# Where the state-space coefficients are computed: tables and coefficients pause in some slots of a two-layer decoder kernel, and coefficients begin 15 slots ahead instead of 9

## The chip, the core and the metric

The kernel runs on one core of a Trainium2 chip. The core has five engines that run side by side and meet through semaphores: TensorE (PE in the profile, with its weight loads as PEld), VectorE (DVE), ScalarE (ACT), GpSimd (POOL) and SyncE (SP), which here only starts weight loads. The metric is the time of one execution in microseconds (us) on the device. Lower is better.

## What is computed

Two identical layers work on 512 tokens of 1024 channels in float32. Each layer normalises its input, multiplies it with one wide matrix, feeds parts of the product to three mixers, and adds the gated sum back:

```python
def hybrid_layer(x, ...):
    h = rmsnorm(x, norm_g)
    proj = h @ w_in            # 8704 columns, split into the 13 parts below
    (rq, rk, rv, rz, sq, sk, sv, sz, cu, cz, ga, gb, gc) = split(proj)
    y_a = retention(rq, rk, rv, ...) * silu(rz)
    y_b = stick_breaking(sq, sk, sv, ...) * silu(sz)
    y_c = s5_ssm(cu, ssm_a_re, ssm_a_im, ...) * silu(cz)
    merged = sigmoid(ga) * (y_a @ proj_a) + sigmoid(gb) * (y_b @ proj_b) + sigmoid(gc) * (y_c @ proj_c)
    return x + merged @ w_out

def stick_breaking(q, k, v, ...):        # 8 heads of 64, strictly causal
    z = q @ k.T * scale
    log_keep = where(causal, log_sigmoid(-z), 0)
    after = cumsum(log_keep, reverse=True) - log_keep
    return where(causal, exp(log_sigmoid(z) + after), 0) @ v

def s5_ssm(u, a_re, a_im, log_dt, b_re, b_im, c_re, c_im, ...):   # 32 groups, 64 complex states
    dt = exp(log_dt)
    ab = exp(dt * a_re) * (cos(dt * a_im), sin(dt * a_im))        # one complex step per state
    bb = (ab - 1) / a * b                                         # input matrices
    h[t] = ab * h[t-1] + bb @ u[t]
    y = Re(c @ h) + d_skip * u ; return gelu(y) * sigmoid(gelu(y) @ w_glu + b_glu)
```

What matters below is that the state-space mixer needs quantities that depend on parameters alone (powers of `ab`, and matrices built from them with `b` and `c`), so they can be computed at any time before they are used.

## The kernel before

**Matrix products.** All large products are made in float32 as three products of split operands (helper `three`): a high part `wh` of the weights, a low part `wl`, and `hh`, `hl` of the activations. A weight unit of 128x1024 is loaded as `raw` by SP, then ACT makes `wh` (line 318) and DVE makes `wl` (recorded by the helper of line 197, as are all counted instructions). Up to four units are made ahead (`W.fill`).

**Slots.** `layer` cuts the products into pieces, of 24 matmuls of 512 columns as a rule, and issues them in a fixed order, `ORDER`. One pass of the loop over `mains` is a slot. Each layer has 108; in each the slots are counted here from 0. Slots 0 to 11 are the columns `sk`, `sq`, `sv`; 12 to 23 are `sz` and `gb`; 24 to 27 are `cu`; then `cz`, `pb`, `gc` and the rest. Everything else is a generator that is put on a calendar (`spawn`) for a slot and is advanced there: in a slot come first the generators due, with their matmuls, then the slot's own piece, then the parts that follow it (`late`), then `W.fill`, and last the background work. Each engine executes its instructions in the order in which they were issued, so an instruction issued late in a slot also stands behind all that came before it on its engine.

**Attention.** `sb_pair` handles two heads at a time; the four pairs begin in slots 11, 15, 19 and 23. For each pair the first slot makes split operands (`qd`, `ks` on ACT, `ql`, `ks` on DVE, and on POOL a memset of `ql` and a copy in `qd`). Then come, slot by slot: scores of the last block of head 0 (tile `z3`); scores of the other blocks of head 0 (`z02`, `z1`); `z3` of head 1 together with the turning of head 0's weights (transposes into `wt`); `z02`, `z1` of head 1; the turning of head 1; the product with `sv` (`sbo`). For each score tile ACT makes two sigmoids, DVE scans one of them (`kp`, line 1051) and multiplies (`w`); the transposes of a turn need all of a head's `w`. So pair 0's first scores are in slot 12, its turns in slots 14 and 16, pair 1's in 18 and 20, pair 2's in 22 and 24, pair 3's in 26 and 28. In slots 15, 19 and 23 the first slot of one pair meets the `z02` and `z1` of the pair before it. Score, turn and transpose results share five PSUM tiles (`ps_sm`).

**Tables and coefficients.** `tables` (layer 0 only) makes the powers of `ab` for both layers with small DVE instructions, into `y`, `fr`/`fi` and `cr`/`ci`; its last two steps, six instructions each, fill `cr` and `ci`. A `Coef` object per layer then makes that layer's matrices: first four loads on ACT's queue (line 672) and eight POOL instructions of 128x512 or 64x512 (`bbr`, `bbi`, `ccr`, `cci`), then four quarters. A quarter is six POOL products and sums (`ab`, `ct`), six DVE instructions (`Tr`, `Ti` from `cr`, `ci`, `fr`, `fi`), six more on POOL (`ca`), and copies. It also puts two generators on the calendar: `transpose_in` (eight transposes on PE and two ACT copies into `win`) and `within` (`pk` on PE, `kk` on DVE, 16 copies into `mt` on POOL and ACT). Quarter q begins no earlier than slot `start + 3 q` and, from quarter 2 on, not before an earlier quarter was used; `start` lies `K["lead"]` slots ahead of the first use of the matrices, which is in slot 33:

```python
starts = [at["cu"] + 3 + K["ssm0"]]      # slot 33
coef.start = starts[0] - K["lead"]       # slot 24
```

Both are the background. After each slot the loop adds background steps while the slot's own estimated load is light, `load["G"] < G_SHARE * load["T"] and load["V"] < V_SHARE * load["T"]` (G is POOL, V is DVE, T is PE). The change is in this condition and in `lead`.

Of the kernel before, what the change touches and what calls it, by code (L numbers as in the profile page):

```python
# [35 lines left out]
K = dict(  # L36

    nw=12, w=4, raw=4, b=48,

    sb0=0, sb_gap=4, ssm0=6, ssm_gap=3, ret0=9, ret_gap=3, x0=-3, x1=2, ret_pre=4, lead=9,  # L40

    g=0.9, v=0.7,

    n1=1, n2=1, q1=1, q2=1, k1=1, k2=2, s1=1, s2=1, s3=1, s4=2, s5=1, s6=1, s7=2, b1=1, b2=1, b3=1,
# [3 lines left out]
G_SHARE, V_SHARE = K["g"], K["v"]  # L48
# [138 lines left out]
def trunk(ctx: ExitStack, tc, x_in, w_in, par_in, bc_in, ng_in, cst_in, rope_in, out):  # L187
    nc = tc.nc
    load = {"V": 0.0, "G": 0.0, "T": 0.0}
# [49 lines left out]
    x1 = dp.tile([S, D], F32, name="x1")  # L239
# [24 lines left out]
    def advance(gen, late):  # L264
        d = next(gen, None)
        if d == 0:
            late.append(gen)
        elif d:
            spawn(gen, now[0] + d)
# [83 lines left out]
    def token_major(lhs, evac):  # L353

        units = []

        def piece(t):
            if not units:
                units.extend(W.take() for _ in range(4))
            ps = pmm()  # L360
            for k in range(8):
                if k == 4 and between:
                    between.pop()()
                w = units[k // 2]
                sl = slice(512 * (k % 2), 512 * (k % 2) + 512)
                three(ps, lhs(k, t), (w[0][:, sl], w[1][:, sl]), k == 0, k == 7)
            if t == NT - 1:
                W.free += 4
            then(evac(t, ps))

        return [lambda t=t: piece(t) for t in range(NT)]
# [109 lines left out]
    G = SSM_GROUPS  # L481
# [328 lines left out]
    def layer(l, last, base):  # L810
# [6 lines left out]
        sq, sk, sv = [], [], [None] * NT  # L817
# [464 lines left out]
        def mk_rhs(k, t):  # L1282
# [7 lines left out]
            sv=token_major(hblock, sv_evac),  # L1290
# [18 lines left out]
        mains, at = [], {}  # L1309
# [7 lines left out]
        def quarters():  # L1317

            q = len(starts) - 1
            if q < 4 and coef.ready >= q and now[0] >= starts[-1]:  # L1320
                spawn(ssm(q), now[0])
                starts.append(now[0] + K["ssm_gap"])
# [10 lines left out]
        def chain(*gens):  # L1333
            for x in gens:
                yield from x

        background = chain(tables(), coef.gen) if l == 0 else coef.gen
        for name, m in mains:
            i = now[0]
            quarters()  # L1340
            late = []
            for gen in due.pop(i, []):
                advance(gen, late)
            m()
            while late:
                advance(late.pop(0), late)
            W.fill()
            while load["G"] < G_SHARE * load["T"] and load["V"] < V_SHARE * load["T"]:
                if next(background, "end") == "end":
                    break  # L1350
                load["G"] += 0.05
            for e in load:
                load[e] = 0.0
            W.free += sum(freed)
            freed.clear()
            now[0] += 1
# [3 lines left out]
    for l in range(L):  # L1360
        base = layer(l, l == L - 1, base)
    while due:
        i = min(due)
# [28 lines left out]
```

## Time and profile before

| | us |
|---|---|
| median of 3 runs | 1310.49 |
| lowest, highest | 1309.92, 1311.50 |
| profiled execution, its own time | 1311.17 |
| its span | 1309.5 |
| PE busy in the span | 1271.7 |
| DVE, ACT, POOL busy | 855.6, 537.6, 382.5 |
| mean granted PE clock | 0.992 |

The page of the profile gives busy time and share by engine; a timeline lists instructions with their start, their length and, in brackets, how long the engine had stood idle before them and what ended that; a view of waits adds these idle times up; a view of windows gives each engine's busy time, with the number of instructions, and the granted TensorE clock, in stretches that one chooses (instructions that reach over an edge count). In the trace a slot can be seen by the matmuls at its start: `z` for scores, `wt` for a turn, `mm` for the slot's own piece. The trace names the scans TENSOR_TENSOR_SCAN; the listing of instructions in the next section names them SCALAR_TENSOR_TENSOR.

### The profile page before, as it was taken

The page shows a single profiled execution, that of the slowest core. Times are in us where ns is not written, and L with a number is a line of the kernel's source. Part 1 is how long each engine was busy: PE and PEld are TensorE (multiplying, and loading weights), DVE is VectorE, ACT ScalarE, POOL GpSimd, SP SyncE. Part 2 cuts the span into 40 slices and gives each one's busy share as a digit, 9 for nine tenths or more (in the row PEclk, how much of TensorE's full clock was granted, in tenths as well). Part 3 has the DMA queues.
Part 4 walks back from the last instruction along what each step waited for, and adds up shares of the span by engine and source line. Part 5 has one row for each costly group of instructions (what it writes and reads, how often), then busy time and mean ns, then how long its engine had stood idle before and what let it go on. Part 6 is the DMA issues. An engine that isn't in the chain of part 4 may idle for free. (4 is left out here: it accounts for less than half of the span.)

```text
span 1309.5 us, 16640 instructions
## 1 busy us (share of the span) xinstructions
PE 1271.7 (97%) x6360; PEld 1048.5 (80%) x6360; DVE 855.6 (65%) x1189; ACT 537.6 (41%) x919; POOL 382.5 (29%) x452
## 2 busy tenths in 40 slices
PE   6989989999999999999999999899999999999998
PEld 5867768788887888888888877788888878888887
DVE  5997678776785438556365576789657844575542
ACT  5445534445343534332244445344534534423311
POOL 3340036638442012000042000584555311210000
PEclk9989989999999999999999999899999999999999
DMA  6232221222322322234433222122241232222342
GB/s 223 90 124 77 65 65 49 81 81 89 119 68 65 104 77 77 81 97 141 161 118 127 81 65 71 43 81 65 84 127 65 65 120 90 65 74 88 97 135 75
DMA packets 37375, 120.05 MB, mean 92 GB/s; under 512 B 4144, under 2 KB 4528, under 8 KB 37296
## 3 DMA queue, kind: packets, MB, share of 16 engines
q1 hardware_dynamic: 29664, 105.40, 25.2%
q10 hardware_dynamic: 7632, 13.59, 3.1%
q8 instruction: 50, 0.82, 0.3%
q14 instruction: 29, 0.24, 0.1%
HBM read 114.78 MB, written 4.19 MB: 91 GB/s over the span
## 5 line engine op out<-in xcount | busy, mean ns | idle before, releaser
L197 DVE TENSOR_TENSOR wl<-raw,wh 128x1024 fp32r<-128x1024 f32 x196 | 251.6, 1294 | 114.6 <-ACT wh L318 111.8
L197 PE MATMUL mm<-hh,wh 128*128 128x512 f32 x640 | 256.0, 400 | 0.0
L197 PE MATMUL mm<-hh,wl 128*128 128x512 f32 x640 | 251.2, 393 | 4.9 <-DVE wl L197 4.9
L197 PE MATMUL mm<-hl,wh 128*128 128x512 f32 x640 | 250.7, 392 | 0.0
L318 ACT ACTIVATE wh<-raw 128x1024 fp32r<-128x1024 f32 x196 | 205.8, 1057 | 86.7 <-PE mm L197 38.9
L197 PE MATMUL mm<-wh,hh 128*128 128x512 f32 x512 | 207.5, 405 | 0.9 <-ACT hh L421 0.9
L197 PE MATMUL mm<-wl,hh 128*128 128x512 f32 x512 | 202.6, 396 | 4.3 <-DVE wl L197 4.3
L197 PE MATMUL mm<-wh,hl 128*128 128x512 f32 x512 | 202.0, 395 | 0.0
L197 PEld LDWEIGHTS mm<-hh,wl 128*128 128x128 f32 x640 | 120.8, 189 | 32.2 <-DVE wl L197 6.3
L197 PEld LDWEIGHTS mm<-hh,wh 128*128 128x128 f32 x640 | 121.0, 189 | 25.1 <-issue 1.6
L197 PEld LDWEIGHTS mm<-hl,wh 128*128 128x128 f32 x640 | 121.0, 189 | 23.5
L197 PEld LDWEIGHTS mm<-wl,hh 128*128 128x128 f32 x512 | 104.5, 204 | 24.5 <-DVE wl L197 7.8
L197 PEld LDWEIGHTS mm<-wh,hh 128*128 128x128 f32 x512 | 104.5, 204 | 19.0 <-ACT hh L421 1.3
L197 PEld LDWEIGHTS mm<-wh,hl 128*128 128x128 f32 x512 | 104.2, 204 | 18.4 <-DVE hl L197 0.3
L1051 DVE TENSOR_TENSOR_SCAN kp<-kp,zero 128x511 f32<-128x511 f32 (+1 forms) x64 | 67.6, 1076 | 26.2 <-ACT kp L1047 26.1
L994 ACT ACTIVATE gate<-mm 128x512 f32<-128x512 f32 x48 | 28.6, 596 | 114.2 <-PE mm L197 114.2
L197 POOL TENSOR_SCALAR ms<-ss 128x8 f32<-128x8 f32 (+3 forms) x56 | 19.1, 341 | 181.5 <-DVE ss L824 100.6
L197 POOL TENSOR_TENSOR rs<-ms,mhalf 128x8 f32<-128x8 f32 (+3 forms) x56 | 64.6, 1154 | 4.7
L1033 POOL CAST qd<-qd 64x512 fp32r<-64x512 f32 x16 | 16.3, 1016 | 134.1 <-ACT qd L1028 133.7
L822 ACT ACTIVATE sq<-mm 128x512 f32<-128x512 f32 x32 | 19.0, 593 | 84.6 <-PE mm L197 84.5
L197 PE MATMUL mm<-wl,mgh 128*128 128x512 f32 x128 | 50.1, 391 | 0.2
L197 PE MATMUL mm<-wh,mgh 128*128 128x512 f32 x128 | 49.9, 390 | 0.0
(253 smaller groups left out, 2263.2 us busy)
## 6 DMA issues: line engine op xcount, KB each, us to landing
raw<-in_w SPq DMA_DIRECT2D x196, 512.0 KB, 3.5
x<-in_x SPq DMA_DIRECT2D x8, 256.0 KB, 7.3
rope<-in_rope ACTq DMA_DIRECT2D x8, 256.0 KB, 3.7
xh<-in_x ACTq DMA_DIRECT2D x8, 256.0 KB, 4.4
x<-xh ACTq DMA_DIRECT2D x8, 256.0 KB, 2.0
xh<-x ACTq DMA_DIRECT2D x8, 256.0 KB, 4.6
out<-xh ACTq DMA_DIRECT2D x8, 256.0 KB, 2.1
gB<-in_ng SPq DMA_DIRECT2D x2, 256.0 KB, 5.8
```

Of the source, the lines that this page charges most:

```text
L197: return f(*a, **k)
L318: ACT(wh, raw, AF.Copy)
L822: ACT(s2, ps, AF.Square)
L994: ACT(sg, ps, AF.Sigmoid)
L1033: nc.gpsimd.tensor_copy(out=qd[h][o, :], in_=qd[h][r, :])
L1051: nc.vector.tensor_tensor_scan(v, v, zero1.to_broadcast([P, n - 1]), 1.0, ALU.mult, ALU.add)
```

## The change

`lead` goes from 9 to 15, so that `start` moves from slot 24 to slot 18 in both layers. And no background step is issued in a set of slots: the slot before pair 0's first and that slot itself (10 and 11), and the six slots from pair 3's first (23 to 28).

```diff
-    sb0=0, sb_gap=4, ssm0=6, ssm_gap=3, ret0=9, ret_gap=3, x0=-3, x1=2, ret_pre=4, lead=9,
+    sb0=0, sb_gap=4, ssm0=6, ssm_gap=3, ret0=9, ret_gap=3, x0=-3, x1=2, ret_pre=4, lead=15,
...
         background = chain(tables(), coef.gen) if l == 0 else coef.gen
+
+        first = at["sv"] + 3 + K["sb0"]
+        turn = first + 3 * K["sb_gap"]
+        quiet = {*range(first - 1, first + 1), *range(turn, turn + 6)}
         for name, m in mains:
...
-            while load["G"] < G_SHARE * load["T"] and load["V"] < V_SHARE * load["T"]:
+            while i not in quiet and load["G"] < G_SHARE * load["T"] and load["V"] < V_SHARE * load["T"]:
                 if next(background, "end") == "end":
                     break
```

No instruction is added or taken away. These are the places where instructions move.

DVE in layer 0, slots 10 to 12, as the difference: `sqk` ends slot 10, `ql` and `ks` are pair 0's operands of slot 11, the four `wl` the weights of slots 12 to 15, `kp` and `w` pair 0's first scan and product of slot 12, and `dbl`<-`cr` the start of the last two steps of the tables.

```order
 L197 TENSOR_SCALAR sqk<-T_882,par_193 128x128 x2
+L197 TENSOR_TENSOR ql_922<-sqk,qd_918 64x512
+L197 TENSOR_TENSOR ks_920<-sqk,ks_920 64x512
+L197 TENSOR_TENSOR ql_923<-sqk,qd_919 64x512
+L197 TENSOR_TENSOR ks_921<-sqk,ks_921 64x512
+L197 TENSOR_TENSOR wl<-raw,wh 128x1024 x4
+L1051 SCALAR_TENSOR_TENSOR kp<-kp,zero_85 128x511
+L197 TENSOR_TENSOR w_1018<-w_1018,kp 128x511
 L197 TENSOR_TENSOR dbl_605<-cr 128x128
 L197 TENSOR_TENSOR dbl_606<-ci 128x128
```

The last 12 table instructions moved from ahead of pair 0's operands to behind its first scan and product, in slot 12; on ACT and POOL the four loads and the eight `bbr`/`bbi`/`ccr`/`cci` instructions moved behind the same point, into slots 12 and 13.

POOL in layer 0, before: from pair 2's operands (slot 19) over pair 3's (slot 23) to the first products of quarter 0 (slot 24).

```order
L1030 MEMSET ql_1454 64x512
L1033 COPY qd_1450<-qd_1450 64x512
L1030 MEMSET ql_1455 64x512
L1033 COPY qd_1451<-qd_1451 64x512
L1030 MEMSET ql_1724 64x512
L1033 COPY qd_1720<-qd_1720 64x512
L1030 MEMSET ql_1725 64x512
L1033 COPY qd_1721<-qd_1721 64x512
L197 TENSOR_TENSOR ab_1855<-bbr,y_re 128x512
L197 TENSOR_TENSOR ct<-bbi,y_im 128x512
L197 TENSOR_TENSOR ab_1855<-ab_1855,ct 128x512
```

The same engine now, from pair 1's last operand (slot 15) to the first products for `ca` (slot 21).

```order
L1033 COPY qd_1179<-qd_1179 64x512
L197 TENSOR_TENSOR ab_1448<-bbr,y_re 128x512
L197 TENSOR_TENSOR ct<-bbi,y_im 128x512
L197 TENSOR_TENSOR ab_1448<-ab_1448,ct 128x512
L197 TENSOR_TENSOR ab_1449<-bbr,y_re 128x512
L197 TENSOR_TENSOR ct<-bbi,y_im 128x512
L1030 MEMSET ql_1463 64x512
L1033 COPY qd_1459<-qd_1459 64x512
L1030 MEMSET ql_1464 64x512
L1033 COPY qd_1460<-qd_1460 64x512
L197 TENSOR_TENSOR ab_1449<-ab_1449,ct 128x512
L751 COPY ca<-ccr 64x8x16
```

Five of quarter 0's products moved from behind pair 3's operands to between pair 1's and pair 2's; the sixth, with the `ca` copies, stands behind pair 2's, and the six products for `ca` and four of quarter 1 follow, all ahead of pair 3's operands. Layer 1 has the same move.

ACT in layer 0 now, slots 21 and 22: `ybh` is the split of pair 1's result, `win` the two copies behind the eight transposes of quarter 0, `wt` the copies of pair 2's first turn.

```order
L1048 ACTIVATE w_1533<-z_1607 128x256
L318 ACTIVATE wh<-raw 128x1024
L994 ACTIVATE gate<-mm 128x512
L284 ACTIVATE ybh<-sbo 128x512
L729 ACTIVATE win_1745<-T_1688 128x512
L729 ACTIVATE win_1747<-T_1693 128x512
L1047 ACTIVATE kp<-z_1698 128x512
L1048 ACTIVATE w_1749<-z_1698 128x512
L1074 ACTIVATE wt_1755<-wt 128x512
L1076 ACTIVATE wt_1534<-wt 128x256
```

The two `win` copies, with their transposes on PE, moved from slot 27 to slot 22, behind a `ybh` that waits for DVE; on DVE, `Tr` and `Ti` (six instructions) moved from slots 25 and 26 to the ends of slots 20 and 21, ahead of that `sbo`.

## Rows read from the trace of the kernel before

**Rows 1.** The page, part 1: busy us, share of the span, instructions.

```profile
PE 1271.7 (97%) x6360; PEld 1048.5 (80%) x6360; DVE 855.6 (65%) x1189; ACT 537.6 (41%) x919; POOL 382.5 (29%) x452
```

**Rows 2.** The waits of PE: engine, line, waited for: us in total, times, longest.

```profile
PE wt L1068 <- DVE w L197: 13.5, 8, 3.1
PE mm L197 <- DVE wl L197: 9.2, 7, 3.3
```

**Rows 3.** Windows: start:end, length, busy (count) of PE, PEld, DVE, ACT, POOL; clock, DMA.

```profile
90.82:97.65 6.83, 5.19 (x12) 4.12 (x13) 5.64 (x6) 4.69 (x6) 2.53 (x3) 0.50 0.06 8
...
186.39:193.22 6.83, 4.82 (x16) 4.27 (x17) 6.53 (x7) 0.98 (x2) 3.19 (x4) 0.50 0.17 49
```

**Rows 4.** Windows as before, one slot each, from its first matmul to the next slot's.

```profile
86.91:99.98 13.07, 8.98 (x29) 6.62 (x29) 11.23 (x9) 4.97 (x6) 6.20 (x6) 0.74 0.38 124
736.18:742.24 6.06, 6.06 (x29) 4.82 (x28) 5.87 (x6) 3.59 (x5) 0.00 (x0) 1.00 0.62 197
137.37:144.47 7.10, 7.10 (x39) 5.87 (x37) 4.85 (x6) 3.80 (x7) 0.00 (x0) 1.00 0.04 14
181.93:197.30 15.37, 9.89 (x39) 8.69 (x37) 11.08 (x10) 3.50 (x6) 7.58 (x7) 0.78 0.22 68
206.65:214.05 7.40, 7.40 (x39) 7.05 (x37) 6.57 (x8) 3.15 (x9) 4.14 (x3) 1.00 0.00 0
222.55:230.63 8.08, 7.14 (x35) 5.29 (x33) 7.25 (x10) 3.55 (x8) 6.04 (x8) 1.00 0.43 135
824.18:839.30 15.12, 9.64 (x38) 8.59 (x37) 11.08 (x10) 3.50 (x6) 7.58 (x7) 0.77 0.22 70
```

**Rows 5.** Timeline of PE: start, length, instruction [idle before <- what ended it].

```profile
152.58 1.20 PE L1068 MATMUL wt<-ident,w 128*128 128x128 f32 x9 [0.68 <-DVE w L197]
185.68 0.30 PE L1068 MATMUL wt<-ident,w 128*128 128x128 f32 x1 [3.07 <-DVE w L197]
188.40 2.18 PE L1068 MATMUL wt<-ident,w 128*128 128x128 f32 x9 [2.41 <-DVE w L197]
207.19 1.26 PE L1068 MATMUL wt<-ident,w 128*128 128x128 f32 x10
225.42 0.50 PE L197 MATMUL mm<-hh,wl 128*128 128x512 f32 x1 [0.79 <-DVE wl L197]
```

**Rows 6.** Windows of DVE alone: length, busy (count, those at the edges too), clock, DMA.

```profile
71.92:73.41 1.49, 1.42 (x7) 1.00 0.00 0
74.53:76.78 2.25, 2.18 (x8) 1.00 0.02 4
78.95:86.02 7.07, 6.90 (x13) 1.00 0.31 107
...
145.87:152.52 6.65, 6.35 (x10) 1.00 0.20 54
176.72:188.34 11.62, 11.29 (x10) 0.92 0.17 52
743.13:746.98 3.85, 3.64 (x7) 1.00 0.05 20
205.81:209.67 3.86, 3.79 (x8) 1.00 0.00 0
```

**Rows 7.** Timeline of POOL: the first and the last of quarter 0's six products; the first `ct` for `bbr`.

```profile
79.16 1.61 POOL L197 TENSOR_TENSOR ct<-br,co_re 128x512 f32<-128x512 f32 x1 [8.62 <-DMA br<-in_bc]
...
179.10 1.40 POOL L197 TENSOR_TENSOR ab<-bbr,y_re 128x512 f32<-128x512 f32 x1
...
186.53 1.52 POOL L197 TENSOR_TENSOR ab<-ab,ct 128x512 f32<-128x512 f32 x1
```

**Rows 8.** Timeline: ACT's table load and `win` copies; PE's slot-14 turn in layer 1.

```profile
95.55 1.28 ACT L1047 ACT_TABLE_LOAD   x1
...
214.89 1.12 ACT L729 ACTIVATE win<-T 128x512 f32<-128x512 f32 x2
...
749.38 1.26 PE L1068 MATMUL wt<-ident,w 128*128 128x128 f32 x10
```

## The prediction

> **What bounds the kernel now.** I began with the page's busy shares. PE is busy for 1271.7 us of a 1309.5 us span [rows 1], so the end is set by PE: the change can win only time in which PE stands idle or runs at half clock. The view of PE's waits tells why it stands idle: turns (`wt`) that wait for the attention's last product `w`, 13.5 us in 8 waits with 3.1 the longest, and pieces that wait for a weight's low part `wl`, 9.2 us in 7 [rows 2]. Both are made by DVE. I then looked for stretches in which the granted clock is down, and found it at 0.50 (the lower level, 1.2 GHz) from 90.82 to 97.65 and from 186.39 to 193.22 [rows 3], each time after such waits; the second has a counterpart in layer 1. PE's work in such a stretch, 5.19 and 4.82 us, would need half the time at the upper level, so each costs 2.6 or 2.4 us on top of the wait.
>
> Slot by slot, against a like slot that is undisturbed [rows 4]: slot 12 of layer 0 takes 13.07 us where layer 1's takes 6.06, so 7.0 are lost. Slot 24 takes 15.37 and 15.12 where slot 26, with the same matmuls, takes 7.40: 8.0 and 7.7 are lost. Slot 28 takes 8.08; a slot with a turn and one piece is slot 18's 7.10 less its `z3`, which is the 0.54 from 206.65 to 207.19 [rows 4, 5], so 6.56, and 1.5 are lost in each layer. These are some 26 us in all, and all of it lies in the region of the change.
>
> The causes are two. In slot 12 the last 12 table instructions stand ahead of pair 0's operands on DVE and run beside POOL's products of layer 0's matrices: from 78.95 to 86.02 they fill 6.90 of 7.07 us [rows 6, 7], where like steps alone take 1.49 (six 128x128) and 2.25 (six 128x256) [rows 6]. In slot 24 the turn waits 3.07 and 2.41 for `w` [rows 5]: the chain from `ql` to the last `w` takes 11.62 us in slot 23 and 6.65 in slot 19 [rows 6]. Slot 23's is the one with six POOL products of 128x512 beside it, from 179.10 to 186.53 plus 1.52 [rows 7]. So a product costs DVE (11.62 - 6.65) / 6 = **0.83 us**, if DVE then reads two operands from on-chip memory. This is the price on which most of the sum rests.
>
> **The change part by part.** No instruction is added, so PE's own work stays, and only waits and clock move.
>
> *Slot 24, both layers.* No POOL product is issued in slots 23 to 28, and those issued before are early enough to be done. The chain should fall from 11.62 to 6.65, and the turn's waits of 3.07 and 2.41 with the half-clock stretch behind them should go. What is late next is a `w` by some 0.2, as in the turn with 0.68 [rows 5], of which slot 23's `pk` covers a part. Gain 7.8 in layer 0, 7.5 in layer 1. A bound from below is the two waits alone with the clock left as it is, about 5.5.
>
> *Slot 28.* The 0.79 for `wl` and the stretched second turn [rows 5] come from the same products and from `Tr`/`Ti` on DVE. With both gone 1.5 is won in each layer; the bounds are 0.8 (only the wait) and 1.5.
>
> *Slots 12 to 14, layer 0.* Slot 12's 7.0 go, since the tables no longer stand ahead of pair 0's operands. But the 12 instructions, at least 1.49 + 2.25 = 3.7 us, now stand behind pair 0's first `w`, ahead of the rest of head 0, and slot 14's turn waits for that. In layer 1, where nothing stands there, its last `w` ends at 746.98 [rows 6] and its turn begins at 749.38 [rows 8]: 2.4 of room. So 3.7 - 2.4 = 1.3 are late if DVE runs free. It won't: the `bbr`/`bbi`/`ccr`/`cci` products, which stood beside the tables before, now stand behind the same point. With five of them beside two-operand work the turn comes 1.3 + 5 x 0.83 = 5.5 late, and after a wait like that the clock drops as in the two stretches above [rows 3], 2.6 more: 8.1 in place of 7.0, a **loss of 1.1**. Bounds: 1.3 alone without a drop of the clock, a gain of 5.7; or six products, ACT's 1.28 table load [rows 8] in the chain and a whole stretch of 6.83 at half clock (3.4), together 11, a loss of 4. I take the upper part since the products are queued just there.
>
> *Slots 16 and 20, both layers.* The turn of slot 20 already comes 0.68 late [rows 5], so each product beside it counts in full. Quarter 0's first product is released in slot 15 and meets the last scans of pair 0, and its sixth stands behind pair 2's operands in slot 19. One product each, 0.8 per slot, so 1.6 lost per layer (bounds 0 and 1.49, the length of a product, from (186.53 + 1.52 - 179.10) / 6 [rows 7]).
>
> *Slot 22, both layers.* This is a new meeting. The `ca` products (six) run beside slots 20 and 21 on DVE, 6 x 0.83 = 5.0, and `Tr`/`Ti` come at the ends of these slots, 3.86 where they run free [rows 6]. DVE has 7.10 - 4.85 = 2.25 of room in a slot like 18 [rows 4], so 6.75 in three. So pair 1's `sbo` is 8.9 - 6.75 = 2.1 late, `ybh` waits for it on ACT, and the two `win` copies (1.12 together [rows 8]) stand behind `ybh`. The third `wt` of pair 2's first turn needs a PSUM tile of `ps_sm` which the first of these copies sets free. PE waits 2.1 + 0.6, and I take **2.5 per layer** (bounds 1 and 3.5, since ACT may have the rest of its slot to catch up, or may have its own copies of `wt` late as well).
>
> *What moves at no price.* The eight `T` transposes and the 16 `pk` go from slot 27 to slots 22 and 23 with the same PE time. The `mt` copies and the later quarters come earlier and hide behind PE as before, since from slot 29 on the order is that of before. Pair 3's POOL operands in slot 23 no longer have products behind them; ahead of them stand quarter 1's, which are due a slot before.
>
> Sum: layer 0 is -1.1 - 1.6 - 2.5 + 7.8 + 1.5 = +4.1, layer 1 is -1.6 - 2.5 + 7.5 + 1.5 = +4.9, so 9.0 us are won. The profiled execution took 1311.17, 1.67 of it outside its span, and would take 1302.2. It lies 0.68 above the median, so on the scale of the runs I forecast 1310.49 - 9.0 = **1301.5**.
>
> **The rivals.**
>
> *The products hardly reach PE.* Slot 14 costs 1.0 and slot 22 costs 0.5, both without a change of clock, and the gain grows by 7.1 + 2 x 2.0 to 20: 1290.4. For it speaks that DVE has 2.25 of room in an average slot, against it that the turn at 152.58 waits without any product beside it [rows 5]. Chance 0.13.
>
> *Slot 22's wait halves the clock as well.* At 186.39 a wait of 3.07 with one of 2.41 went with a drop [rows 3, 5], and 2.5 is near that. A whole stretch costs 6.83 / 2 = 3.4 in each layer, which leaves 9.0 - 6.8 = 2.2: 1308.3, or 1304.9 if it happens in one layer. Chance 0.18.
>
> *Slower: a product holds DVE for its whole length.* The price would be 1.49 in place of 0.83, which is 0.66 more for each: 3.3 in slot 14, 0.7 in each of the four waits of slots 16 and 20, 4.0 in slot 22 of each layer and then also its half clock, 3.4. That is 3.3 + 2.8 + 8.0 + 6.8 = 20.9 against the 9.0: 11.9 slower, 1322.4. It decides once a product costs the chain more than about 1.2. Slot 23's six products added 4.97 to the chain and not 8.9 [rows 6, 7], which speaks against it; but there the chain also has parts that read PSUM, which need not pay, and a denser stretch of two-operand work would pay more. Chance 0.09.
>
> The Trainium skill, page "SBUF — State Buffer", section "Summary: rules for kernel authors", has this rival as a rule: if a DVE instruction has two SBUF inputs while a GpSimd instruction reads SBUF, the one that is issued second fully blocks until the first finishes. By that rule the sum would be the 1322.4 above, and moving products from behind pair 3 to between the other pairs would be a bad exchange. The trace agrees that the two hinder each other, but has 0.83 for a product of 1.49.
>
> That the change doesn't do what it says is excluded by the order of instructions: the products, the tables and the operands do change places in both layers.
>
> **How the numbers follow.** Forecast 0.60, with its own range of 1297 to 1306 from the bounds of slots 14 and 22; the rivals 0.13, 0.18 and 0.09. About 0.2%, 2.6 us, is what a measurement of this kernel can tell from no change, so "the same" is 1307.9 to 1313.1. Faster: nearly all of the forecast (0.58), the first rival, and the one-layer half of the second (0.05), 0.76. The same: the second rival with both layers (0.11) and the rest of the forecast, 0.13. Slower: the third, and 0.02 for a second rival with further waits, 0.11. The range reaches from the first rival's time to a little above the second's, 1290 to 1310; it leaves out the third and about half of the first.
>
> **What the next profile would show.** Right: in both layers slot 24 near 7.4 with no wait of 2 us or more and the clock whole, slot 28 near 6.6, a `wt` wait for `w` of some 5 us in slot 14 of layer 0 with a half-clock stretch behind it, waits of about 1.5 at slots 16 and 20, and in slot 22 a `wt` that waits about 2.5 for ACT's `win`. Wrong: if slots 12 to 14 of layer 0 are clean (the products reach nothing there), if slot 22 has a half-clock stretch, if slot 24 still waits though no product stands beside slot 23, or if anything from slot 29 on has become longer, since nothing of that is in my sum.

## The result, and the profile after

The changed kernel takes 1303.55 us (median of 6 runs), the kernel before 1310.37 beside it: a ratio of 0.9944, 95% interval 0.9933 to 0.9955, so 6 to 9 us faster. One of the six executions took 2571.09 us, for a reason that no run shows; the ratio leaves it out, and the median without it is 1303.42. The profiled execution took 1303.42 in place of 1311.17, its span is 1301.7 in place of 1309.5.

First the page, part 1 (busy us, share, instructions), which answers to [rows 1]:

```profile
PE 1267.4 (97%) x6360; PEld 1048.0 (81%) x6360; DVE 853.3 (66%) x1189; ACT 537.5 (41%) x919; POOL 391.3 (30%) x452
```

Then PE's waits (us in total, times, longest), which answer to [rows 2]:

```profile
PE wt L1068 <- DVE w L197: 12.3, 8, 6.0
...
PE mm L197 <- DVE wl L197: 4.3, 4, 1.6
PE wt L1068 <- ACT win L729: 4.1, 2, 2.1
```

The instruction counts are those of before. The wait for `w` has hardly shrunk in total, but it has moved: its longest is 6.0 where it was 3.1, the one for `wl` has halved, and a new one is there, for ACT's `win`.

Now slot by slot, windows of the changed kernel as in [rows 4] (start:end, length, busy of PE, PEld, DVE, ACT, POOL, clock): slots 12 to 14 of layer 0, then its slots 16, 20, 22, 24 and 28, then slots 16, 20, 22 and 24 of layer 1, and last the two stretches in which the clock is down.

```profile
86.32:115.27 28.95, 22.30 (x98) 17.94 (x97) 24.16 (x30) 11.69 (x18) 9.89 (x9) 0.88 0.37 128
121.90:130.44 8.54, 7.32 (x39) 5.90 (x37) 8.33 (x9) 3.54 (x6) 7.72 (x5) 1.00 0.19 61
153.26:162.45 9.19, 7.51 (x38) 5.97 (x37) 8.88 (x9) 3.60 (x6) 5.65 (x4) 1.00 0.18 57
171.55:181.86 10.31, 8.22 (x47) 6.73 (x45) 9.48 (x10) 4.88 (x9) 7.59 (x8) 1.00 0.16 52
189.18:196.78 7.60, 7.60 (x38) 7.11 (x37) 6.91 (x11) 3.28 (x6) 5.21 (x7) 1.00 0.45 140
220.47:227.14 6.67, 6.67 (x36) 5.42 (x34) 5.14 (x5) 2.50 (x7) 0.00 (x0) 1.00 0.61 182
...
758.74:767.28 8.54, 7.32 (x38) 5.91 (x37) 8.33 (x9) 3.54 (x6) 7.72 (x5) 1.00 0.21 61
790.10:799.10 9.00, 7.51 (x38) 5.97 (x37) 8.69 (x9) 3.60 (x6) 6.24 (x5) 1.00 0.18 58
808.20:820.07 11.87, 9.83 (x46) 7.87 (x45) 10.29 (x10) 4.88 (x9) 9.03 (x8) 0.86 0.15 44
827.39:834.99 7.60, 7.60 (x38) 7.11 (x37) 6.91 (x11) 3.28 (x6) 5.21 (x7) 1.00 0.49 140
...
104.10:110.93 6.83, 4.59 (x16) 3.82 (x17) 6.52 (x9) 1.93 (x3) 0.00 (x0) 0.50 0.00 0
814.07:817.49 3.42, 3.42 (x10) 2.65 (x9) 3.31 (x3) 1.75 (x4) 3.34 (x3) 0.50 0.00 0
```

For comparison, windows of the kernel before that were not shown: its slots 12 to 14, 16 and 20 of layer 0. The first of them begins with a wait of 0.79 for `ks`, so that this wait is counted in it.

```profile
86.91:113.70 26.79, 22.70 (x98) 17.93 (x98) 20.29 (x21) 11.47 (x18) 6.20 (x6) 0.87 0.27 88
120.33:128.28 7.95, 7.34 (x39) 5.90 (x38) 6.55 (x9) 3.59 (x6) 0.52 (x1) 1.00 0.25 69
151.10:159.11 8.01, 7.33 (x39) 5.90 (x37) 6.01 (x8) 3.54 (x6) 0.00 (x0) 1.00 0.31 82
```

Slot 24 has become 7.60 in both layers, with PE busy all of it; slot 28 is 6.67. Against that stand slots 12 to 14 (28.95 against 26.79, where layer 1 takes 19.78), slot 16 (+0.6), slot 20 (+1.2, +1.0) and slot 22, which without its transposes (0.79) is 2.4 longer than the 7.10 of an undisturbed slot in layer 0 and 4.0 in layer 1. The difference between the layers is the second half-clock stretch.

Where the time of slots 14 and 22 goes is seen in the timelines of the changed kernel (start, length, instruction, [idle <- what ended it]): the turn of slot 14, where the wait for `w` now stands, then DVE, ACT and PE of slot 22.

```profile
105.69 0.48 PE L1068 MATMUL wt<-ident,w 128*128 128x128 f32 x1 [6.00 <-DVE w L197]
...
173.60 0.69 DVE L197 TENSOR_TENSOR Ti<-ct,ct 128x512 f32<-128x512 f32 x1
174.21 0.68 DVE L197 TENSOR_TENSOR sbo<-sbo,silu 128x512 f32<-128x512 f32 x1
...
174.93 0.63 ACT L284 ACTIVATE ybh<-sbo 128x512 fp32r<-128x512 f32 x1 [2.59 <-DVE sbo L197]
175.47 1.07 ACT L729 ACTIVATE win<-T 128x512 f32<-128x512 f32 x2
...
176.10 0.33 PE L1068 MATMUL wt<-ident,w 128*128 128x128 f32 x1 [2.09 <-ACT win L729]
```

In slot 22 `Ti` stands ahead of the product into `sbo`; `ybh` waits for that, the `win` copies wait behind `ybh`, and PE's third `wt` waits for the tile that the first copy frees.

### The profile page after: what moved, and what is told of

It reads as the page before. It is cut to its first block, busy times and chain, and to the rows that moved or that the text cites. A ratio compares the mean times of both kernels' runs of the same rounds, so it can differ in the third digit from the quotient of the medians.

```text
span 1301.7 us, 16635 instructions
## 1 busy us (share of the span) xinstructions
PE 1267.4 (97%) x6360; PEld 1048.0 (81%) x6360; DVE 853.3 (66%) x1189; ACT 537.5 (41%) x919; POOL 391.3 (30%) x452
## 5 line engine op out<-in xcount | busy, mean ns | idle before, releaser
L1051 DVE TENSOR_TENSOR_SCAN kp<-kp,zero 128x511 f32<-128x511 f32 (+1 forms) x64 | 59.8, 955 | 21.3 <-ACT kp L1047 21.2
L197 PE MATMUL mm<-wh,mgl 128*128 128x512 f32 x128 | 49.9, 390 | 0.0
```

What stands on the lines that cost most here:

```text
L197: return f(*a, **k)
L1051: nc.vector.tensor_tensor_scan(v, v, zero1.to_broadcast([P, n - 1]), 1.0, ALU.mult, ALU.add)
```

## Undoing one part: the early start alone, the pause without slots 10 and 11

```diff
-        quiet = {*range(first - 1, first + 1), *range(turn, turn + 6)}
+        quiet = set()
```

> Only lead goes from 9 to 15; the pauses are left out. My theory: the earlier start brings the costs in slots 16, 20 and 22 that the changed kernel has (together 4.2 us in layer 0 and 5.5 in layer 1 in its trace), and without the pause the rest of quarter 1 comes in slots 24 to 26 and keeps a part of the loss of slots 24, 26 and 28. Slot 12 of layer 0 loses its 7.0 as in the kernel before. Together about as long as the kernel before or longer, 1308 to 1316 us. Rival, that the early start alone brings the gain (the pauses being needless): 1301 to 1305, with slot 24 near 7.6.

It took 1312.57 us, 1.0014 (1.0004 to 1.0023) of the kernel before: slightly slower, as the theory had it. But one step of that theory fell. Of this run, windows of slots 24 and 26 of layer 0, and then PE's timeline in slot 26:

```profile
186.96:194.84 7.88, 7.61 (x39) 7.11 (x37) 7.51 (x10) 3.28 (x6) 6.51 (x6) 1.00 0.32 85
204.20:219.03 14.83, 10.77 (x47) 8.94 (x46) 9.21 (x11) 4.23 (x11) 10.34 (x9) 0.77 0.00 0
```

```profile
211.16 0.48 PE L1068 MATMUL wt<-ident,w 128*128 128x128 f32 x1 [3.64 <-ACT win L729]
```

Slot 24 is 7.88: it is the earlier start that empties slot 23, not the pause. What the pause does is to keep quarter 1's transposes and `win` copies out of slot 26, where they make the same wait as in slot 22, 3.64 us in each layer, with a half-clock stretch. So the early start pays only together with the pause in slots 23 to 28. The pause without the early start was not run.

```diff
-        quiet = {*range(first - 1, first + 1), *range(turn, turn + 6)}
+        quiet = {*range(turn, turn + 6)}
```

> The changed kernel with background work let into slots 10 and 11 again; slots 23 to 28 stay quiet and lead stays 15. My theory: slots 12 to 14 of layer 0 go back to the kernel before, where slot 12 loses 7.0 and slot 14 nothing, in place of the 9.2 that the changed kernel's trace shows; all else as in the changed kernel. 2.2 us faster than it: about 1301.3. Rival, that the first pause is a gain (it would be if the loss at slot 12 were larger than the one at slot 14): 1305 or more.

1301.11 us, 0.9923 (0.9906 to 0.9940): 2.4 below the changed kernel's median and near the 2.2 expected, but only in part for the reason that I gave. In this run's view of waits PE waits for `ks` in slot 12, where the changed kernel waits 6.00 and 0.65 in slot 14; the half-clock stretch comes with either. Behind that row stand windows of this run: slots 12 to 14 of layer 0 with that wait, slot 20 of layer 0, and slot 22 of layer 1.

```profile
PE z L197 <- DVE ks L197: 4.1, 1, 4.1
...
86.19:113.94 27.75, 23.17 (x99) 17.92 (x98) 21.15 (x25) 11.48 (x18) 3.13 (x5) 0.88 0.26 84
151.94:162.75 10.81, 9.13 (x39) 7.18 (x38) 10.50 (x11) 3.59 (x6) 7.27 (x5) 0.84 0.17 57
807.40:817.66 10.26, 8.22 (x47) 6.73 (x45) 9.43 (x10) 4.88 (x9) 8.67 (x8) 1.00 0.17 51
```

Slots 12 to 14 win 1.2 (27.75 in place of 28.95), not 2.2. The rest comes from slots that I expected to stay as they were: slot 20 of layer 0 loses 1.6, with a new half-clock stretch, and slot 22 wins 1.3 in layer 0 (9.00) and 1.6 in layer 1, where the same wait of 2.04 comes without a half-clock stretch. So the pause in slots 10 and 11 is a loss of about 1.2 by these two traces; that the total came out as forecast is luck. The interval also overlaps that of the changed kernel (0.9933 to 0.9955), as do those of coef_wait and gate_only below: gaps of about 2 us to it are not settled by the times alone.

## What makes slot 14 late: the tables or the products beside them

Layer 0's loads and its six products were held until the end of slot 14, so that the 12 table instructions alone stand behind pair 0's first product.

```diff
+            while l == 0 and now[0] < 14:
+                yield
             raw = [bt(n) for n in ("br", "bi", "ccr", "cci")]
```

> The changed kernel, but layer 0's four loads and six bbr/bbi products wait until the end of slot 14, so that only the 12 table instructions stand behind pair 0's first product. My theory (the POOL products beside it, not the 12 instructions, make slot 14's turn late): the 12 take some 3.5 us in place of 8.85, the turn waits 1.3 in place of 6.0 + 0.65 and no half-clock stretch follows, 7.9 us won there; the products meet slot 15's scans instead and cost up to 2.5 at slot 16's turn. Net gain 4 to 8 over the changed kernel, 1295.5 to 1299.5. Rival, that the 12 instructions themselves are the delay: the wait stays above 4 and the time within 2 us of the changed kernel.

1301.72 us, 0.9926 (0.9911 to 0.9941): 1.8 won, not 4 to 8. Slot 14's half of the theory held: it is 8.59 long, with waits of 0.25 and 0.80. The products' half was too small: slot 16 now takes 14.24, and has taken over the waits (2.71 and 1.31) and the stretch at half clock. Windows of this run's slots 14 and 16, and its timeline of PE in slot 16:

```profile
99.14:107.73 8.59, 7.54 (x38) 5.97 (x37) 7.09 (x10) 3.54 (x6) 2.42 (x2) 1.00 0.67 189
114.36:128.60 14.24, 10.22 (x39) 8.20 (x37) 11.71 (x11) 3.54 (x6) 12.09 (x10) 0.76 0.20 54
```

```profile
117.75 0.30 PE L1070 MATMUL wt<-ident,w 128*128 128x128 f32 x1 [2.71 <-DVE w L197]
```

So the products are what costs, wherever they meet a chain that a turn waits for; the tables alone cost about 1.

## Slot 22: the wait goes, and comes back in slot 24

```diff
-            spawn(transpose_in(), now[0] + K["w1"])
+            spawn(transpose_in(), now[0] + (5 if q == 0 else K["w1"]))
```

> The changed kernel, but quarter 0's eight transposes and two win copies come in slot 25 and not in slot 22, in both layers. My theory (slot 22's turn waits for a PSUM tile that the first win copy frees, and that copy stands behind ybh): the waits of 2.09 and 2.04 go, with the half-clock stretch of layer 1, worth 1.6; slot 22 comes near 7.1 in both layers, about 5.8 us won, 1297.7. Rival, that slot 22's turn would be late anyway for w, since DVE is behind by the same products: waits of 1 us or more for w in slot 22, and a gain under 2 us.

1303.70 us, 0.9943 (0.9928 to 0.9958): no gain. My theory was right for slot 22 and wrong for the time. Windows of slots 22 and 24 of layer 0, and of slot 24 of layer 1:

```profile
171.56:178.66 7.10, 7.10 (x39) 5.87 (x37) 6.30 (x7) 3.92 (x7) 4.42 (x4) 1.00 0.21 75
185.98:197.26 11.28, 9.29 (x39) 8.21 (x37) 9.01 (x14) 3.50 (x6) 5.66 (x8) 0.85 0.31 94
...
823.92:835.10 11.18, 9.24 (x38) 7.98 (x37) 8.94 (x14) 3.50 (x6) 5.66 (x8) 0.85 0.30 95
```

Slot 22 is down to 7.10, and slot 24 up from 7.60 to 11.28 and 11.18. DVE was behind; in the changed kernel PE waits in slot 22, and that wait gives DVE the time to catch up before slot 24. To see what DVE is behind by, quarter 1 was held until slot 25 as well:

```diff
-            while self.used < q - 1 or now[0] < self.start + K["ssm_gap"] * q:
+            while self.used < q - 1 or now[0] < self.start + (7 if q == 1 else K["ssm_gap"] * q):
...
-        quiet = {*range(first - 1, first + 1), *range(turn, turn + 6)}
+        quiet = {*range(first - 1, first + 1), *range(turn, turn + 2)}
```

> The run win_late (transposes and win copies in slot 25) with quarter 1 not before slot 25, so that its four products are no longer issued in slot 22; slots 25 to 28 are not quiet here, so only slots 22 to 24 are compared. win_late lost in slot 24 what it won in slot 22. Theory A: slot 24's wait for w there (1.19 + 0.80 and a half-clock stretch) comes from quarter 1's four products, which stand beside slot 22's scan, w and wl and lengthen them by about 2.3: without them slot 24 comes to 7.4 to 7.7 in both layers, slot 22 staying at 7.1. Theory B: it comes from DVE being behind by Tr/Ti and quarter 0's ca products: slot 24 keeps a wait above 1.

One execution, 1300.32 us. Slot 22 is 7.10 and slot 24 7.78 in both layers, so theory A holds, with slot 24 a little above its 7.4 to 7.7: four products of quarter 1, which the changed kernel issues in slot 22, stood beside the scan, `w` and `wl` of that slot. Its window of slot 24 in layer 1:

```profile
822.10:829.88 7.78, 7.61 (x39) 7.08 (x38) 7.08 (x11) 3.28 (x6) 5.21 (x7) 1.00 0.45 137
```

## What a POOL product costs DVE

Two kernels add unused POOL instructions to the changed one, behind pair 3's `z02` scan in slot 27 (`kp_last` holds the tile of that scan, `pa` three unused tiles); each was executed once. The edit of the first, without the lines that set these tiles up; the second has other instructions in the same place:

```diff
+            if i == base + 27:
+                GS(out=st("gate", 1), in0=kp_last[0][:, 1:2], scalar1=1.0, scalar2=1.0, op0=ALU.mult, op1=ALU.mult)
+                for _ in range(6 if l == 0 else 6):
+                    if l == 0:
+                        nc.gpsimd.memset(pa[2], 0.0)
+                    else:
+                        GT(out=pa[2], in0=pa[0], in1=pa[1], op=ALU.mult)
```

> The changed kernel with POOL instructions added at slot 27, behind pair 3's scan of z02, whose results nobody uses: in layer 0 six memsets of 128x512, in layer 1 six products of 128x512. DVE has there a product w, a scan, a w and four wl of two operands each. If what hinders DVE is POOL reading the same memory (the Trainium skill, SBUF - State Buffer, Summary: rules for kernel authors, has this as blocking of the second by the first), memsets cost DVE nothing: w 0.69, scan 0.68, w 0.42, wl 1.22 each in layer 0, and the products add about 0.9 each in layer 1, 5 to 6 us over w, scan, w and the four wl. If it is any POOL work, both layers lengthen alike per us of POOL. If a product blocked for 1.49, as the slower case of the prediction had it, layer 1 would be 8.9 longer.

> As probe_mem_prod, but in layer 0 six POOL instructions of 128x512 with one operand read, and in layer 1 twelve products. If it is a matter of turns at the memory (one DVE instruction, then one of POOL), each DVE instruction of two operands lengthens by about one POOL instruction's own time, whatever POOL reads; in layer 1 all seven DVE instructions lengthen, by 0.6 to 1.06 each, and no more than seven products can count, so 12 cost about as much as 7. If it is a share of the bandwidth, one-operand instructions cost about half of a product's 0.9, and the lengthening per DVE instruction goes with its own length.

The timeline of the first kernel: DVE beside memsets (layer 0), DVE beside products (layer 1, the last row the four `wl`), and POOL's six memsets and six products.

```profile
217.33 0.69 DVE L197 TENSOR_TENSOR w<-w,kp 128x511 f32<-128x511 f32 x1
217.94 0.68 DVE L1053 TENSOR_TENSOR_SCAN kp<-kp,zero 128x255 f32<-128x255 f32 x1
218.72 0.43 DVE L197 TENSOR_TENSOR w<-w,kp 128x255 f32<-128x255 f32 x1
...
853.86 1.69 DVE L197 TENSOR_TENSOR w<-w,kp 128x511 f32<-128x511 f32 x1
855.47 1.78 DVE L1053 TENSOR_TENSOR_SCAN kp<-kp,zero 128x255 f32<-128x255 f32 x1
857.36 1.26 DVE L197 TENSOR_TENSOR w<-w,kp 128x255 f32<-128x255 f32 x1
858.54 8.75 DVE L197 TENSOR_TENSOR wl<-raw,wh 128x1024 fp32r<-128x1024 f32 x4
...
217.15 3.46 POOL L1368 MEMSET pc<- 128x512 f32 x6
...
853.71 10.51 POOL L197 TENSOR_TENSOR pc<-pa,pb 128x512 f32<-128x512 f32 x6
```

The timeline of the second: DVE beside the instructions that read one operand (layer 0), DVE's four `wl` beside twelve products (layer 1).

```profile
216.99 0.99 DVE L197 TENSOR_TENSOR w<-w,kp 128x511 f32<-128x511 f32 x1
217.91 1.09 DVE L1053 TENSOR_TENSOR_SCAN kp<-kp,zero 128x255 f32<-128x255 f32 x1
219.10 0.59 DVE L197 TENSOR_TENSOR w<-w,kp 128x255 f32<-128x255 f32 x1
...
859.85 8.97 DVE L197 TENSOR_TENSOR wl<-raw,wh 128x1024 fp32r<-128x1024 f32 x4
```

Memsets cost nothing. Beside products `w` goes from 0.69 to 1.69, the scan from 0.68 to 1.78, the short `w` from 0.43 to 1.26: +1.00, +1.10, +0.83, nearly the same for long and short instructions. That is near to taking turns, with a whole product as POOL's turn: alone one takes 1.07 (the first product of gate_only, shown in the next section, begins while DVE stands idle), and here 10.51 / 6 = 1.75, its own 1.07 and 0.68 more for DVE's turns. With twelve products the four `wl` take 8.97, with six and two of quarter 1 behind them 8.75: twelve products beside seven DVE instructions cost about as much as eight. Instructions of one operand cost less, +0.30, +0.41 and +0.16, though each took 6.44 / 6 = 1.07 there. Here the theory of turns missed, since it had a whole turn "whatever POOL reads"; the smaller cost, least for the shortest instruction, is nearer to the rival, a share of the bandwidth. What such an instruction does to DVE stays open.

The Trainium skill, "SBUF — State Buffer", "Summary: rules for kernel authors", says that where a DVE instruction has two SBUF inputs and a GpSimd instruction reads SBUF, the second one to issue fully blocks until the first finishes. The runs come near to that for products (0.83 to 1.10 beside a product's 1.07), and memsets, which read nothing and so fall outside the rule, cost nothing; for the one-operand instructions they show 0.16 to 0.41, less than a full block.

## The same gain without an earlier start

If the products beside slot 23's chain are the whole cause of slot 24's loss, it is enough to start them a little later. In the kernel before, one small POOL instruction that reads DVE's copy of the last turn was put ahead of quarter 0's products; `lead` stays 9 and nothing pauses.

```diff
+                turned_last[0] = wt13[h]
...
+    def after_turn():
+        t = st("gate", 1)
+        GS(out=t, in0=turned_last[0][:, 0:1], scalar1=1.0, scalar2=1.0, op0=ALU.mult, op1=ALU.mult)
...
+            if q == 0:
+                after_turn()
             ab = [bt("ab0"), bt("ab1")]
```

> The kernel before (lead 9, no pause) with one small POOL instruction put ahead of quarter 0's products in each layer: it reads one column of the copy that DVE makes of slot 24's turn, so the products start there, near 196 us, and not behind pair 3's operands near 179. Nothing begins earlier and no slot pauses. My theory (slot 24's loss is the six products beside slot 23's chain, and nothing else): the chain takes 6.65 again, slot 24 comes to 7.4 to 7.6 in both layers with no half-clock stretch, 15.3 us won; the products, Tr/Ti and the ca products then share slots 24 to 28, where DVE stands idle 12.9 us against about 14 that they ask, and cost 0 to 4 per layer there. 1295.5 to 1303. Rival (pair 3's operands or its start by themselves make slot 24 late, or the products only move the loss to slots 26 and 28): 1306 to 1311.

1301.38 us, 0.9930 (0.9915 to 0.9944), 2.2 below the changed kernel's median. POOL's instruction waits until 189.67 (its timeline), and slot 24 takes 8.47 (its window); most of what that has above 7.4 is a wait of 0.74 for `w`, of the kind that slot 20 of the kernel before has too (0.68). Slot 23's chain takes 6.80 again, from 177.73 to 184.53, where the kernel before had 11.62. So slot 24 wins 6.9 and 6.7, not the 15.3 in all; slot 27 gives a part back, with 10.93 where the kernel before takes 8.50.

```profile
189.67 0.19 POOL L197 TENSOR_SCALAR gate<-wt 128x1 f32<-128x1 f32 x1 [9.64 <-DVE wt L1083]
189.82 1.07 POOL L197 TENSOR_TENSOR ab<-bbr,y_re 128x512 f32<-128x512 f32 x1
```

```profile
182.95:191.42 8.47, 7.73 (x39) 7.21 (x37) 6.26 (x8) 3.28 (x6) 1.75 (x3) 1.00 0.40 124
```

Then layer 0's loads and products were held until the end of slot 13, with the tables left ahead of pair 0's operands:

```diff
+            while l == 0 and now[0] < 13:
+                yield
             raw = [bt(n) for n in ("br", "bi", "ccr", "cci")]
```

> The kernel of the run gate_only with one more edit: layer 0's four loads and six bbr/bbi products wait until the end of slot 13, while the 12 last table instructions stay in slot 10, ahead of pair 0's operands, where DVE stands idle 3.8 us if nothing is put there. My theory: the tables take 3.5 without products beside them, so slot 12 loses under 1 us; the products run near 98 to 106, beside the end of slot 13's chain, and cost slot 14 under 1. Slots 12 to 14 lose at most 2 where the kernel before loses 7.0 and the changed one 9.2: 5 to 7 faster than gate_only, 1289 to 1298. Rival, that a wait for ks stays above 3 in slot 12 because of the tables alone, or that slot 14 or 16 takes the loss over: within 2 us of gate_only.

1295.28 us, 0.9881 (0.9864 to 0.9897), 6.1 below the run before. Windows of this run, slots 12 to 14 and slot 27 of layer 0. The first takes 19.78, PE busy throughout:

```profile
87.01:106.79 19.78, 19.78 (x98) 16.13 (x97) 17.74 (x18) 11.47 (x18) 9.58 (x6) 1.00 0.51 161
200.71:214.31 13.60, 11.49 (x58) 9.40 (x57) 13.15 (x15) 8.12 (x18) 12.73 (x12) 0.75 0.13 39
```

The second row is slot 27, the largest loss left, where `pk` waits 1.64 for a PSUM tile. Two more kernels moved `pk`, and then the transposes too, to slot 28:

```diff
-            spawn(within(), now[0] + K["w2"])
+            spawn(within(), now[0] + K["w2"] + (q == 0))
...
-            spawn(transpose_in(), now[0] + K["w1"])
+            spawn(transpose_in(), now[0] + (3 if q == 0 else K["w1"]))
```

> The kernel of the run gate_tables with quarter 0's 16 pk products (and what follows them) one slot later, in slot 28. In gate_tables the largest loss left is slot 27, 13.60 us in layer 0 (with a half-clock stretch) and 10.97 in layer 1 where the kernel before takes 8.5: pk waits 1.64 for a PSUM tile that DVE's copy of slot 26's turn sets free. My theory: in slot 28 that copy is long done, so both waits go and with them the half-clock stretch of layer 0; 4 to 7 us won, 1288 to 1291. Rival: DVE is behind there by the products and Tr/Ti, so the wait comes back as one for w in slot 28's turn: within 2 us of gate_tables.

> As gate_pk, with quarter 0's eight transposes in slot 28 as well, so that nothing of quarter 0 needs a PSUM tile in slot 27. The transposes' own wait (0.47 and 0.49, for the last ab product) goes too. My theory: 1 us faster than gate_pk, 1287 to 1290. Rival: five tiles are then asked for in slot 28, and its turn waits for one as slot 22's did in the changed kernel: slower than gate_pk by 1 to 4.

1294.12 us (0.9873, 0.9858 to 0.9888) and 1293.73 us (0.9870, 0.9853 to 0.9886). The half-clock stretch is gone, but only about 1.2 and 0.4 were won where 4 to 7 and 1 were expected, and the intervals of gate_tables, gate_pk and gate_pk_T overlap. Slot 27 is 8.59 in gate_pk, so my step for it held; but the time is the rival's, within 2 us of gate_tables. A part of the wait comes back further on, 0.34 for `w` in slot 28's turn and 0.54 at the `sbo` products behind slot 28, which wait for DVE's copy of its turn; where the rest of the gain goes was not followed. Of gate_pk, the window of slot 27, then the timeline of PE:

```profile
200.89:209.48 8.59, 8.13 (x43) 7.42 (x41) 8.26 (x9) 8.00 (x17) 8.24 (x9) 1.00 0.19 62
```

```profile
210.72 1.20 PE L1078 MATMUL wt<-ident,w 128*128 128x128 f32 x9 [0.34 <-DVE w L197]
...
220.21 0.54 PE L197 MATMUL sbo<-wt,sv 128*64 128x384 f32 x2 [0.54 <-DVE wt L1085]
```

Both are faster than the kernel before and the changed one.

## Why the prediction was right, point by point

| term (us, + is won) | predicted, layers 0 and 1 | measured, layers 0 and 1 |
|---|---|---|
| slot 24 | +7.8, +7.5 | +7.8, +7.5 |
| slot 28 | +1.5, +1.5 | +1.4, +1.5 |
| slots 12 to 14 | -1.1 | 26.79 - 28.95 = -2.2 |
| slot 16 | -0.8, -0.8 | -0.6, -0.6 |
| slot 20 | -0.8, -0.8 | -1.2, -1.0 |
| slot 22 | -2.5, -2.5 | -2.4, -4.0 |
| sum | 9.0 | 6.2 |

The spans differ by 7.8, so 1.6 lies outside these slots: slot 12 is reached 0.6 earlier, and behind slot 28 the time from slot 29 of layer 0 to slot 12 of layer 1 is 505.20 in place of 505.55 and from slot 29 of layer 1 to the end 436.37 in place of 436.81. The medians differ by 6.8. The forecast was 1301.5 with 9.0 won, and the time came out 2 us above it. That it is so near is in part luck: the terms miss by 2.8, and 1.6 came back where the prediction had put nothing.

**What held.** The losses of slots 24 and 28 went, the tables moved from slot 12 to slot 14's turn and cost more there, and the new wait in slot 22 was the one named, ended by ACT's `win` copy, 2.09 and 2.04 for the 2.5 forecast. gate_only shows by itself that slot 24's loss is the six products beside slot 23's chain: starting them, and what follows them, later brought the chain from 11.62 to 6.80 and slot 24 from 15.37 to 8.47. Nothing from slot 29 on became longer.

**What was mis-sized.** Slot 22 in layer 1: the rival "slot 22's wait halves the clock as well" came true in one layer (a half-clock stretch there was among the prediction's own signs of being wrong), for 3.42 us of busy PE, a cost of 1.7 and not 3.4, since the stretch was half as long as those before. Slot 20 cost 0.2 to 0.4 more per layer. Slots 12 to 14 cost 1.1 more, twice the loss that was forecast: there the wait was 6.65 and not 5.5, and all six products of 128x512 ran beside the chain, from 91.86 to 100.14, where I had counted five.

**The reason given for slot 24** was worded wrongly. I put the gain down to no products being issued in slots 23 to 28; lead15_only has no pause and slot 24 at 7.88. The early start moves the products away; the pause keeps `win` out of slot 26.

**The price of a product** was 0.83 as an average over one chain. The slower rival had a product hold DVE for its whole length, 1.49, and the prediction said that the rows spoke against it. For products of two operands the probes come near to the mechanism of that rival; its price was wrong, because 1.49 was read beside DVE's work and already had DVE's turns in it. Alone a product is 1.07, and DVE pays 0.83 to 1.10 per instruction that meets one. That is below the 1.2 from which the prediction let the rival decide, so it could not have come to 1322. One of the arguments against it was wrong too: slot 23's chain has no parts that read PSUM, since `ql`, `ks`, `kp` and `w` are all made from tiles in SBUF, on-chip memory that POOL's products read too.

**What the prediction did not see.** Quarter 1's four products in slot 22 also make DVE late, and PE's wait in slot 22 hides that from slot 24; only win_late and win_late_hold brought it out. The prediction had these products among the things that move at no price.

## What to carry to other kernels

Where PE waits for a chain on DVE, look at what POOL does beside the chain before moving anything earlier: a later start, tied by a one-column read to the end of the chain, gave at least as much (1301.4) as the earlier one (1303.6, and 1301.1 without the pause in slots 10 and 11), and clearly more once the products beside the tables were held back too (1295.3). Take a contention price from an instruction that runs alone and one that meets the other engine, not from a mean of both. And when a wait is removed, look at the same engine two slots on: twice here (slot 22 to 24, slot 27 to the products behind 28) at least a part of it came back because the engine was behind, not the one instruction. The first of these was tested, by win_late_hold; the second is only read from the waits.

## What the runs showed of the hardware that I had not expected

Beside POOL's products of two operands DVE pays nearly a whole product per instruction, whatever its own length: a short `w` of 0.43 pays 0.83 beside products, a `wl` of 1.22 pays (8.97 - 4.90) / 4 = 1.02, with 4.90 as the four take alone. POOL writing without reading (memset) disturbs nothing, and reading one operand costs 0.16 to 0.41. The same kind of wait in slot 22, 2.09 in layer 0 and 2.04 in layer 1, went with a stretch at half clock only in layer 1, and in late_quiet the 2.04 of layer 1 went without one; what decides that the runs do not tell.
